# RWKV recurrence with two head pairs in step, mLSTM output projection in two rounds, and more row buffers, in a two-layer hybrid decoder step on one Trainium2 core

## The chip, the core and the metric

The kernel runs on one core of one Trainium2 chip. The engines that matter are TensorE (PE, with its weight loads shown as PEld), VectorE (DVE), ScalarE (ACT), GpSimd (POOL) and SyncE (SP), which here only issues DMAs. The metric is the device time of one execution in microseconds, the median of several runs.

## The reference

One inference step of a decoder trunk with two layers and D = 1024. A prompt of 512 tokens and 8 sample sequences of 4 tokens run through the same weights, so the kernel works on 544 columns. Each layer is a half SwiGLU (d_ff 2816), a mixer, and another half SwiGLU; mixer 0 is RWKV-7 time mixing (16 heads of 64), mixer 1 is mLSTM (8 heads, DV 128, DK 64). All is fp32.

```
def trunk(x, ...):
    for i in range(2):
        x = x + 0.5 * swiglu(rmsnorm(x), wg, wu, wd)       # "a"
        x = x + mixer_i(rmsnorm(x))
        x = x + 0.5 * swiglu(rmsnorm(x), wg, wu, wd)       # "b"
    return rmsnorm(x), states

def rwkv step(S, r_t, d_t, k_t, v_t, kk_t, b_t):           # per head, S is 64 x 64
    sa = S @ -kk_t
    S = S * d_t + outer(sa, b_t) + outer(v_t, k_t)
    return S, S @ r_t
# then group norm per head, + bonus, * gate, @ wo

def mlstm chunk(C, n, m):                                  # per head
    b = cumsum(logf); Dlog = b_t - b_s + logi_s, causal; m_t = max(b + m, max_s Dlog)
    S = (q k^T) * exp(Dlog - m_t)
    num = exp(b + m - m_t) * (C q) + S v; den likewise with n
    h = num / max(|den|, exp(-m_t))                        # then norm, * sigmoid(o), @ w_out
```

## The kernel before

Activations lie transposed, features on the 128 partitions and tokens along the row, in two parts of columns: PARTS[0] has 256 prompt tokens, PARTS[1] the other 256 and the 32 sample tokens. A dense product takes fp32 weights of 128 x 1024 from memory (`weight`, three raw buffers), splits them into a high and a low part (`split`: a copy on ScalarE, L341, and a subtraction on VectorE, L342) and multiplies in three matmuls (`mm3`, L345 to L347), 24 for one block of 128 output features and one part of columns. The instruction order on each engine comes from a planner that places ready work by priority in a simulated time line; work inside `high_priority` goes ahead of the dense work. PSUM has eight banks of 512 fp32 columns.

**The RWKV stage** runs beside dense work: SwiGLU "a" of part 1 and the projections of both parts, later the output projection and SwiGLU "b" of part 0 (`todo`, handed out by `step`; FILL and FILL2 say after which list entry how many units follow). Its recurrence works on head pairs (16 heads are 8 pairs of 128 partitions) and on 4 chunks of 64 tokens for each part, thus on 16 pairs in all, the second 8 starting from the state of the first. Pair n goes through:

- `rwkv_prep` (decays and scaled keys, bank `pq`),
- `rwkv_quad`: masked products of all four chunks (L907 on PE, mask L909 on DVE into `gm`), then the inverse of a unit triangular matrix by doubling in f16, with bursts of eight 64x64 matmuls (L928 to L960) that alternate with a copy (L938), an addition (L943) and a mask (L924); the result is `tf` (L962). Pairs alternate between two lanes, with one bank each (`b0`, `b1`); `gm`, `xt`, `tf`, `uv` have three buffers,
- `rwkv_tokens` (values transposed, bonus),
- `rwkv_chunk`, four times, each on the state of the one before: L1004/1007, copy L1009, L1012, copies L1013/1014, L1017, state L1022, output L1025/1028, copy L1029. Pair q and pair q - 1 run half a pair apart, each in a bank `pc` of its own,
- `rwkv_sample` in the second half: the 8 sample sequences of this pair, some 15 small products one after another (L1046 to L1100) that all go through the bank `ps`, of which there is one, and end in L1101 and the state's DMA,
- `rwkv_finish`: group norm and gate, three products (L1116, L1120, and the gate's up to L1133) in the bank of the other quad lane, up to L1134. In the second half it needs the sample's output (L1093).

The tiles of the sample recurrence lie in the scope `rw2`, whose memory comes free when the second half's projections (scope `rw1`) are done.

**The mLSTM stage** projects q and k for head pair j + 1 (`mlstm_qk`), while `mlstm_weights`, `mlstm_pair` and `mlstm_heads` work on pair j in banks of their own. `mlstm_weights` loads rows from memory broadcast to all partitions (`qi`, two buffers, L1345; `d`, four buffers, two per pair, L1353) and adds and masks them (L1356). Then come eight gates (`mlstm_gate`, dense, one `og` buffer each), eight products (`mlstm_out`) and the output projection (`project_out`), which for each of 8 output blocks and each part of columns sums over all eight heads and adds to x once (L501).

## Time and profile before

| what | us |
|---|---|
| median of 3 runs (2597.35 to 2598.86) | 2598.71 |
| profiled execution | 2593.75 |
| its span, first to last instruction | 2591.9 |

Durations are those of the profiled execution. L12 is line 12 of the kernel before. Stretches are given in us from the start of the span: dense SwiGLU "a" of part 0 to about 195, the RWKV stage to about 1238, dense work to 1862, the mLSTM stage to about 2176, dense work to the end. The granted clock is the mean share of full speed that PE was given; it has two levels, 1.2 and 2.4 GHz, so 0.75 means half of the time at the lower one. A matmul of fp32 shows as two records, of f16 or of the split parts as one. Matmuls overlap, so what one adds is the distance from its start to the next start, not its duration.

### The profile page before, as it was taken

The numbers are of one execution on the slowest core, as the hardware profiler recorded it, in microseconds if no ns is written. First come the engines' busy times: TensorE is split into PE (matmuls) and PEld (weight loads), VectorE is DVE, ScalarE is ACT, GpSimd is POOL, SyncE is SP. The second block draws the span as 40 slices with busy tenths as digits, with TensorE's granted clock in tenths as the row PEclk, the third lists the DMA queues.
The fourth block names the chain that finished last, engine by engine and source line by source line (L and its number), as shares of the span: only waits on it lengthen the run. The fifth ranks groups of instructions, "written<-read, shape, count | busy, mean of one in ns | idle before, by whom it ended". The sixth has DMA issues, their size and how long they took to land.

```text
span 2591.9 us, 54493 instructions
## 1 busy us (share of the span) xinstructions
PE 2512.9 (97%) x21731; PEld 2342.7 (90%) x21731; DVE 1583.3 (61%) x3266; ACT 1278.1 (49%) x2917; POOL 513.0 (20%) x578
## 2 busy tenths in 40 slices
PE   9998999999899999999999999999998999999997
PEld 8997998888788787889999999999977979999997
DVE  6667786778887687656766544443436645444433
ACT  6555665656666564545555533333335544333322
POOL 1204332332532243323121011110000000111100
PEclk9998999999899899999999999999998979999999
DMA  7564544233232232345555432322232312322232
GB/s 217 183 195 140 160 140 123 82 106 122 70 104 87 88 102 87 118 133 168 163 165 167 133 90 83 96 84 86 86 101 88 89 52 75 97 82 90 86 90 72
DMA packets 101070, 291.65 MB, mean 113 GB/s; under 512 B 12440, under 2 KB 28216, under 8 KB 100816
## 3 DMA queue, kind: packets, MB, share of 16 engines
q1 hardware_dynamic: 100816, 288.18, 36.5%
q8 instruction: 170, 2.79, 0.4%
q14 instruction: 84, 0.69, 0.1%
HBM read 278.76 MB, written 9.38 MB: 111 GB/s over the span
## 4 chain that ended last, share of the span: by engine, by line
PE 87%; DVE 8%; issue 1%; DMA 1%; ACT 1%; POOL 1%; SPq 0%; DVEq 0%; ACTq 0%; POOLq 0%
PE ps L345 17%; PE ps L347 17%; PE ps L346 17%; PE pd L345 7%; PE pd L346 7%; PE pd L347 7%; DVE wl L342 2%; DVE m L662 1%; PE ps L1209 1%; PE ps L1210 1%; PE pq L907 1%; PE ps L1211 1%; PE pc L1025 1%; PE b L907 1%; PE pc L1017 1%
## 5 line engine op out<-in xcount | busy, mean ns | idle before, releaser
L342 DVE TENSOR_TENSOR wl<-wr,wh 128x512 fp32r<-128x512 f32 (+2 forms) x1025 | 719.9, 704 | 482.2 <-ACT wh L341 458.6
L341 ACT CAST wh<-wr 128x512 fp32r<-128x512 f32 (+2 forms) x1025 | 622.6, 609 | 656.1 <-PE ps L346 419.4
L345 PE MATMUL ps<-a,wh 128*128 128x288 f32 (+1 forms) x2384 | 697.4, 293 | 11.0 <-ACT a L393 5.2
L347 PE MATMUL ps<-a,wl 128*128 128x288 f32 (+1 forms) x2384 | 694.0, 291 | 0.1
L346 PE MATMUL ps<-a,wh 128*128 128x288 f32 (+1 forms) x2384 | 687.3, 288 | 0.3
L345 PEld LDWEIGHTS ps<-a,wh 128*128 128x128 f32 x2384 | 452.3, 190 | 14.2 <-ACT a L393 5.7
L346 PEld LDWEIGHTS ps<-a,wh 128*128 128x128 f32 x2384 | 452.1, 190 | 2.3 <-DVE a L394 1.1
L347 PEld LDWEIGHTS ps<-a,wl 128*128 128x128 f32 x2384 | 449.9, 189 | 1.6 <-DVE wl L342 0.5
L417 POOL TENSOR_TENSOR t<-t,t 128x256 f32<-128x256 f32 (+1 forms) x132 | 141.6, 1073 | 862.4 <-ACT wh L341 404.9
L345 PE MATMUL ps<-h,wh 128*128 128x288 f32 (+1 forms) x1056 | 303.9, 288 | 0.0
L346 PE MATMUL ps<-h,wh 128*128 128x288 f32 (+1 forms) x1056 | 303.3, 287 | 0.0
L347 PE MATMUL ps<-h,wl 128*128 128x288 f32 (+1 forms) x1056 | 303.2, 287 | 0.0
L345 PE MATMUL pd<-rk,wh 128*128 128x288 f32 (+1 forms) x656 | 199.1, 304 | 5.8 <-DVE t L477 5.2
L346 PE MATMUL pd<-rk,wh 128*128 128x288 f32 (+1 forms) x656 | 198.7, 303 | 0.8 <-DVE rk L394 0.5
L347 PE MATMUL pd<-rk,wl 128*128 128x288 f32 (+1 forms) x656 | 199.0, 303 | 0.0
L347 PEld LDWEIGHTS ps<-h,wl 128*128 128x128 f32 x1056 | 198.9, 188 | 0.0
L346 PEld LDWEIGHTS ps<-h,wh 128*128 128x128 f32 x1056 | 198.9, 188 | 0.0
L345 PEld LDWEIGHTS ps<-h,wh 128*128 128x128 f32 x1056 | 198.6, 188 | 0.0
L341 ACT CAST h<-t 128x256 fp32r<-128x256 f32 (+1 forms) x132 | 55.3, 419 | 200.2 <-POOL t L417 200.2
L345 PEld LDWEIGHTS pd<-rk,wh 128*128 128x128 f32 x656 | 127.5, 195 | 9.6 <-ACT mx L663 2.9
L346 PE MATMUL pd<-mx,wh 128*128 128x256 f32 (+1 forms) x448 | 134.5, 301 | 1.4 <-DVE mx L664 1.3
L345 PE MATMUL pd<-mx,wh 128*128 128x256 f32 (+1 forms) x448 | 134.3, 301 | 0.7 <-ACT t L712 0.4
(406 smaller groups left out, 4731.2 us busy)
## 6 DMA issues: line engine op xcount, KB each, us to landing
wr<-in_f0a_u_dram SPq DMA_DIRECT2D x44, 512.0 KB, 3.5
wr<-in_f0b_g_dram SPq DMA_DIRECT2D x44, 512.0 KB, 3.5
wr<-in_f0b_u_dram SPq DMA_DIRECT2D x44, 512.0 KB, 3.5
wr<-in_f0a_g_dram SPq DMA_DIRECT2D x43, 512.0 KB, 3.5
wr<-in_f0b_d_dram SPq DMA_DIRECT2D x24, 512.0 KB, 3.6
wr<-in_f1a_g_dram SPq DMA_DIRECT2D x22, 512.0 KB, 3.4
wr<-in_f1a_u_dram SPq DMA_DIRECT2D x22, 512.0 KB, 3.5
wr<-in_f1b_g_dram SPq DMA_DIRECT2D x22, 512.0 KB, 3.5
```

The lines of the kernel that those rows point to most:

```text
L341: self.S.copy(dst_h, src)
L342: self.V.tensor_tensor(dst_l, src, dst_h, op=ALU.subtract)
L345: self.T.matmul(out, wh, xh, start=start, stop=False)
L346: self.T.matmul(out, wh, xl, start=False, stop=False)
L347: self.T.matmul(out, wl, xh, start=False, stop=stop)
L417: self.G.tensor_tensor(s, s, w, op=ALU.mult)
L662: V.scalar_tensor_tensor(m, d, self.vec("mu", c * 8 + k), xn, op0=ALU.mult, op1=ALU.add)
L907: T.matmul(pg[:, i * P:(i + 1) * P], xc[R[h], i].rearrange("p x t -> p (x t)"), arc[R[h], i].rearrange("p x t -> p (x t)"), start=True, st ...
L1017: T.matmul(pn[R[h], :64], xt[:, h * 64:(h + 1) * 64], uv[:, h, :], start=True, stop=True)
L1025: T.matmul(py[R[h], :64], uv[:, h, :], gm[:, 1 - h, 64:128], start=True, stop=st is None)
L1209: T.matmul(pss[q][:n, :], xs[k][0][:, ts], wt(cs)[0], start=k == 0, stop=False)
L1210: T.matmul(pss[q][:n, :], xs[k][0][:, ts], wt(cs)[1], start=False, stop=False)
```

## The change

Two head pairs go through the recurrence in step, as a double pair m (four for each half). `rwkv_quad` handles eight chunks at once: its bursts have 16 matmuls instead of 8, its ops twice the columns, and it writes one PSUM tile of two banks (`wide_bank`, one buffer) in place of the two lanes. The masked products of L907 alternate between the two heads, each with a bank. `rwkv_chunk` does one chunk of both pairs; its output gathers in a bank over the four chunks and is copied once. `rwkv_finish` takes the bank `ps`. Buffers change: `gm`, `xt`, `tf`, `uv` hold two double pairs; a2 tiles 10 instead of 8, mixing buffers 19 instead of 21; two more k projections come before the first quad, FILL and FILL2 stay. A double pair's quad is issued at the first chunk of the one before, its preparation two chunks later, the samples at the first two chunks, both finishes at the fourth.

In mLSTM the gates have six `og` buffers, heads 0 and 1 are multiplied before the last two gates, and the output projection runs in two rounds, over heads 0 to 3 and 4 to 7, each with half of the weights' columns and an addition to x of its own. `qi` has three buffers and `d` six.

```diff
@@ -26,10 +26,10 @@
 TT = TP + TS
 HA = TP // 2
-OFF=(20000,20000)
-SOFF = 20000
+OFF = 20000
+NMX = 19
 NT1 = 3
-NOG = 8
+NOG = 6
...
+ND = NPAIR // 2
+NA2 = 10
...
-            for k in range(KT):
+            for k in range(len(xs)):
                 c = slice(k * mw, (k + 1) * mw)
-                self.mm3(ps, *wt(c), xs[k][0][:, hs], xs[k][1][:, hs], k == 0, k == KT - 1)
+                self.mm3(ps, *wt(c), xs[k][0][:, hs], xs[k][1][:, hs], k == 0, k == len(xs) - 1)
...
-    def project_out(self, name, xs):
-        for m in range(KT):
-            def evac(i, hs, ps, m=m):
-                self.V.tensor_tensor(self.x[m][:, hs], ps, self.x[m][:, hs], op=ALU.add)
-            self.dense(self.a[name][m], xs, evac)
+    def project_out(self, name, xs, halves=1):
+
+        n = KT // halves
+        for ks in (range(h * n, (h + 1) * n) for h in range(halves)):
+            xk = [xs(k) for k in ks]
+            for m in range(KT):
+                def evac(i, hs, ps, m=m):
+                    self.V.tensor_tensor(self.x[m][:, hs], ps, self.x[m][:, hs], op=ALU.add)
+                self.dense(self.a[name][m][:, ks.start * P:ks.stop * P], xk, evac)
...
-                self.d, self.quad = {}, {}
-                self.chain = [self.bank("pc", 2) for _ in range(2)]
-                self.nhm = {"mx": 21, "hm": 8}
+                self.d, self.quad, self.st = {}, {}, {}
+                self.chain, self.chain_y = [self.bank("pc", 2) for _ in range(2)]
+                self.nhm = {"mx": NMX, "hm": 8}
...
-                    with self.tc.high_priority(OFF[0]):
-                        for n in (0, 1):
-                            self.rwkv_ahead(n)
-                            self.rwkv_square(n)
+                    with self.tc.high_priority(OFF):
+                        self.rwkv_ahead(0)
+                        self.rwkv_square(0)
                     for q, f in enumerate(second):
                         f()
                         self.step(FILL2.get(q, 0))
-                    with self.tc.high_priority(OFF[0]):
-                        for n in (0, 1):
-                            self.rwkv_value(n)
+                    with self.tc.high_priority(OFF):
+                        self.rwkv_value(0)
+                        self.rwkv_ahead(1)
                     first, second = self.rwkv_first(1)
                     self.todo += first
-                    self.rwkv_slots(0, 2 * NPAIR - 4)
+                    self.rwkv_slots(0, 10)
                     self.todo += second
-                    self.rwkv_slots(2 * NPAIR - 4, 2 * NPAIR)
+                    self.rwkv_slots(10, 16)
                 self.nhm = {"hm": 16}
                 with self.scope("rw2", nps=0):
-                    self.rwkv_slots(2 * NPAIR, 2 * NPAIR + 2)
+                    with self.tc.high_priority(OFF):
+                        self.rwkv_value(ND)
+                    self.rwkv_slots(16, 17)
                     self.todo += self.rwkv_out(0) + self.ffn_units(*after, 0)
-                    self.rwkv_slots(2 * NPAIR + 2, 4 * NPAIR + 2)
+                    self.rwkv_slots(17, 32)
...
-        return ([lambda: self.rwkv_norm(i)] + low[:4] + self.rwkv_project("r", 0, i) + k[:3],
-                k[3:] + low[4:] + self.rwkv_project("v", 3, i))
+        return ([lambda: self.rwkv_norm(i)] + low[:4] + self.rwkv_project("r", 0, i) + k[:5],
+                k[5:] + low[4:] + self.rwkv_project("v", 3, i))
...
+    def rwkv_value(self, m):
+        if m < 2 * ND:
+            uv = self.rp("uv", 2, [P, 1024]).rearrange("p (a c h v) -> p a c h v", a=2, c=4, h=2)
+            for a in range(2):
+                self.rwkv_tokens(2 * (m % ND) + a, m // ND, self.d[m][a]["v"], uv[:, a])
+            self.quad[m] += (uv,)
 
     def rwkv_slots(self, t0, t1):
 
+        for t in range(t0, t1):
+            m, c = divmod(t, 4)
+            i, j = divmod(m, ND)
+            with self.tc.high_priority(OFF):
+                if c == 0:
                     self.rwkv_square(m + 1)
+
+                    if m + 1 != ND:
+                        self.rwkv_value(m + 1)
+                if c == 2:
                     self.rwkv_ahead(m + 2)
+                if i and c in (0, 1):
+                    self.rwkv_sample(2 * j + c, self.d[m][c])
+                self.rwkv_chunk(m, c)
+                if c == 3:
+                    for a in range(2):
+                        self.rwkv_finish(2 * j + a, i, m)
+            self.step(-(-len(self.todo) // (t1 - t)))
...
+        return {"xc": xc, "xs": xs, "arc": arc, "ars": ars, "pc": pc, "y": k, "v": v}
+
+    def rwkv_quad(self, ds):
         V, S, G, T = self.V, self.S, self.G, self.T
         R = (slice(0, 64), slice(64, 128))
+        W = 8 * CH
+        pb = lambda: self.wide_bank()
+        h16 = lambda tag, w=W: self.rp(tag, 1, [P, w], F16)
+        q8 = lambda t: t[:, :W].rearrange("p (q t) -> p q t", q=8)
+        q4 = lambda t: t[:, :W].rearrange("p (a c t) -> p a c t", a=2, c=4)
+        wide = lambda m: m.unsqueeze(1).to_broadcast([P, 8, m.shape[-1]])
         em = lambda l: self.em16[:, l * CH:(l + 1) * CH]
         id16 = em(6)
         def each(f):
+            for q in range(8):
+                for g in range(2):
+                    f(R[g], slice(q * CH, (q + 1) * CH), slice(W + q * CH, W + (q + 1) * CH))
+        flat = lambda t: t.rearrange("p x t -> p (x t)")
+        gm = self.rp("gm", 2, [P, 2048]).rearrange("p (a c h t) -> p a c h t", a=2, c=4, h=2)
+        xt = self.rp("xt", 2, [P, 1024])
+        mask = self.maskg.unsqueeze(1).to_broadcast([P, 4, P])
+        for a, d in enumerate(ds):
+            xc, arc = d["xc"], d["arc"]
+            pg = pb()
             for i in range(4):
+                for h in range(2):
+                    T.matmul(pg[:, (1 - h) * 512 + i * P:(1 - h) * 512 + (i + 1) * P], flat(xc[R[h], i]), flat(arc[R[h], i]),
+                             start=True, stop=True)
+            for h in range(2):
+                V.tensor_tensor(gm[:, a, :, h, :], pg[:, h * 512:(h + 1) * 512].rearrange("p (c t) -> p c t", c=4), mask, op=ALU.mult)
+
+        for a, d in enumerate(ds):
+            px = self.bank("pq", 1)
             for i in range(4):
+                T.transpose(px[:, i * P:(i + 1) * P], flat(d["xc"][:, i]), self.ident)
+            S.copy(xt[:, a * 512:(a + 1) * 512], px)
...
-                V.tensor_tensor(both, both, pd, op=ALU.add)
-            else:
-                V.tensor_tensor(ti, ti, pd[:, :W], op=ALU.add)
+            for x in range(2 if l < 5 else 1):
+                z = slice(x * W, (x + 1) * W)
+                V.tensor_tensor(both[:, z], both[:, z], pd[:, z], op=ALU.add)
...
+    def wide_bank(self):
+        self.n += 1
+        return self.psum.tile([P, 1024], F32, tag="b", name=f"b_{self.n}", bufs=1)
...
+    def rwkv_chunk(self, m, c):
+        V, S, T = self.V, self.S, self.T
         R = (slice(0, 64), slice(64, 128))
+        gm, tf, xt, uv = self.quad[m]
+        ds = self.d[m]
+        st = self.st.get((m - ND) if c == 0 else m)
+        arc, pc = [d["arc"] for d in ds], [d["pc"][:, c:c + 1] for d in ds]
+        col = lambda a: slice(a * 64, (a + 1) * 64)
+        reg = lambda z: self.chain[:, z * P:(z + 1) * P]
+        pairs = [(a, h) for a in range(2) for h in range(2)]
         if st is not None:
+            sp = self.rp("sp", 1, [P, P])
+            for a in range(2):
+                S.activation(sp[:, col(a)], st[:, col(a)], AF.Copy, scale=pc[a])
+        pr, pu, pn = reg(c % 2), reg(2), reg(3)
+        for a in range(2):
             for h in range(2):
+                T.matmul(pr[R[1 - h], col(a)], gm[R[h], a, c, 1 - h, 0:64], uv[R[h], a, c, h, :], start=True, stop=st is None)
+            for h in range(2 if st is not None else 0):
+                T.matmul(pr[R[1 - h], col(a)], arc[a][R[h], c, 0, :], st[R[h], col(a)], start=False, stop=True)
+        rhs = self.rp("sm", 3, [P, P])
+        V.tensor_copy(rhs, pr)
+        for a in range(2):
+            for g in (1, 0):
+                T.matmul(pu[R[g], col(a)], tf[R[g], (a * 4 + c) * CH:(a * 4 + c + 1) * CH], rhs[R[g], col(a)], start=True, stop=True)
+        two = lambda t: t.rearrange("p (a v) -> p a v", a=2)
+        V.tensor_copy(uv[R[1], :, c, 0, :], two(pu[R[1]]))
+        S.copy(uv[R[0], :, c, 1, :], two(pu[R[0]]))
+        for a, h in pairs:
+            z = (a * 4 + c) * P + h * 64
+            T.matmul(pn[R[h], col(a)], xt[:, z:z + 64], uv[:, a, c, h, :], start=True, stop=True)
+        sn = self.rp("stp", ND, [P, P]) if m < ND and c == 3 else self.rp("sm", 3, [P, P])
+        for a in range(2):
+            if st is None:
+                V.tensor_scalar(sn[:, col(a)], pn[:, col(a)], pc[a], None, op0=ALU.mult)
+            else:
+                V.scalar_tensor_tensor(sn[:, col(a)], pn[:, col(a)], pc[a], sp[:, col(a)], op0=ALU.mult, op1=ALU.add)
+        out = lambda a: slice(a * 4 * CH + c * CH, a * 4 * CH + (c + 1) * CH)
+        py = self.chain_y
+        for a in range(2):
             for h in range(2):
+                T.matmul(py[R[h], out(a)], uv[:, a, c, h, :], gm[:, a, c, 1 - h, 64:128], start=True, stop=st is None)
+            for h in range(2 if st is not None else 0):
+                T.matmul(py[R[h], out(a)], st[R[h], col(a)], arc[a][R[h], c, 1, :], start=False, stop=True)
+        if c == 3:
+            for a in range(2):
+                S.copy(ds[a]["y"][:, :HA], py[:, a * HA:(a + 1) * HA])
+        self.st[m] = sn
...
-        pb = lambda: self.bank(f"b{(j + 1) % NSTREAM}", 1)
+        pb = self.ps
...
-                ogs = [self.mlstm_gate(h, xs, rs) for h in range(8)]
-                ys = [self.mlstm_out(h, og) for h, og in enumerate(ogs)]
-                self.project_out("m_out", ys)
+                ogs = [self.mlstm_gate(h, xs, rs) for h in range(NOG)]
+                ys = [self.mlstm_out(h, ogs[h]) for h in range(8 - NOG)]
+                ogs += [self.mlstm_gate(h, xs, rs) for h in range(NOG, 8)]
+                self.project_out("m_out", lambda h: ys[h] if h < len(ys) else self.mlstm_out(h, ogs[h]), 2)
...
-        qi = self.unit("qi", 2)
+        qi = self.unit("qi", 3)
...
-        wS = [self.unit("d", 4) for _ in range(2)]
+        wS = [self.unit("d", 6) for _ in range(2)]
```

## Rows read from the trace of the kernel before

**Rows 1.** The page: busy microseconds by engine, and TensorE's granted clock in 40 slices.

```profile
PE 2512.9 (97%) x21731; PEld 2342.7 (90%) x21731; DVE 1583.3 (61%) x3266; ACT 1278.1 (49%) x2917; POOL 513.0 (20%) x578
...
PEclk9998999999899899999999999999998979999999
```

**Rows 2.** Table by stretches: PE, PEld, DVE, ACT, POOL busy; clock, DMA, GB/s.

```profile
398.00:640.00 242.00, 237.62 (x2694) 206.17 (x2688) 182.89 (x392) 145.99 (x372) 75.49 (x90) 0.99 0.35 106
640.00:824.00 184.00, 169.88 (x1731) 147.86 (x1731) 151.00 (x318) 116.66 (x312) 68.50 (x94) 0.91 0.30 92
824.00:1184.00 360.00, 353.27 (x3882) 293.60 (x3881) 250.80 (x593) 198.84 (x515) 119.74 (x137) 0.96 0.35 106
...
1238.00:1862.00 624.00, 623.13 (x4863) 622.43 (x4861) 317.10 (x575) 258.44 (x492) 71.52 (x72) 1.00 0.38 116
...
1982.00:2007.00 25.00, 15.86 (x87) 11.25 (x83) 14.86 (x58) 15.01 (x53) 2.04 (x2) 0.71 0.31 100
...
2097.00:2126.00 29.00, 26.75 (x106) 17.64 (x106) 12.67 (x48) 11.09 (x50) 2.52 (x2) 0.58 0.17 51
2126.00:2176.00 50.00, 49.42 (x381) 48.95 (x380) 31.39 (x62) 22.12 (x46) 0.00 (x0) 0.97 0.24 75
```

**Rows 3.** Timeline of PE, 912 to 916 us: start, duration, instruction.

```profile
912.10 0.28 PE L347 MATMUL pd<-xs,wl 128*128 128x256 f32 x1
912.31 0.31 PE L936 MATMUL b<-ti,e 64*64 64x64 f16 x8
912.55 0.75 PE L1120 MATMUL b<-a,c_c_rw 128*128 128x288 f32 x2
...
915.35 0.31 PE L940 MATMUL b<-p1s,ti 64*64 64x64 f16 x8
915.49 0.29 PE L942 MATMUL b<-ti,p1s 64*64 64x64 f16 x8
915.71 0.41 PE L345 MATMUL b<-a,a 128*128 128x288 f32 x1
```

**Rows 4.** Timeline of PE, the same product in two orders.

```profile
569.09 1.16 PE L907 MATMUL b<-a 64*128 64x128 f32 x8
570.17 0.33 PE L1012 MATMUL pc<-sm,tf 64*64 64x64 f32 x4
...
1958.41 1.16 PE L1365 MATMUL pS<-q,k 64*128 64x128 f32 x16
1959.50 0.44 PE L1393 MATMUL px<-c_c_all,k 128*128 128x128 f32 x2
```

**Rows 5.** Two lines of the sample recurrence: ns min/median/max, first and last start.

```profile
L1101 DVE TENSOR_TENSOR s<-s,ps x8: 686/688/689, 866.2 to 1180.4; 128x512 f32<-128x512 f32 x8
...
L1048 DVE TENSOR_TENSOR sa<-ps,c_c_rw x16: 205/216/217, 824.0 to 1142.5; 64x64 f32<-64x64 f32 x16
```

**Rows 6.** First mask and last op of the quads, same columns.

```profile
L909 DVE TENSOR_TENSOR gm<-b,c_c_rw x16: 660/691/692, 338.2 to 1063.3; 128x512 f32<-128x512 f32 x16
...
L962 DVE TENSOR_TENSOR tf<-ti,b x16: 402/419/422, 398.4 to 1117.9; 128x256 f32<-128x256 f16 x16
```

**Rows 7.** Timelines of PE, ACT and DVE: one rwkv_finish; then its last line.

```profile
908.98 0.75 PE L1116 MATMUL b<-rk,c_c_rw 128*128 128x288 f32 x2
...
910.07 0.42 ACT L1118 ACTIVATE a<-b 128x288 f32<-128x288 f32 x1
...
913.34 0.50 ACT L756 ACTIVATE a<-b,epsc 128x288 f32<-128x288 f32 x1 [0.31 <-PE b L1120]
...
918.24 0.45 DVE L1134 TENSOR_TENSOR rk<-rk,b 128x288 f32<-128x288 f32 x1
...
L1134 DVE TENSOR_TENSOR rk<-rk,b x16: 410/430/455, 479.2 to 1185.0; 128x256 f32<-128x256 f32 x8, 128x288 f32<-128x288 f32 x8
```

**Rows 8.** DVE in mLSTM: a wait for rows; the projection's evacuations.

```profile
1992.81 0.62 DVE L1356 SCALAR_TENSOR_TENSOR d<-d,cols,c_c_ml 128x128 f32<-128x128 f32 x2 [1.58 <-DMA d<-dc]
...
L501 DVE TENSOR_TENSOR x<-ps,x x16: 424/437/458, 2132.7 to 2176.1; 128x256 f32<-128x256 f32 x8, 128x288 f32<-128x288 f32 x8
```

More of the change, by code (lines that the diff above doesn't have):

```diff
@@ L640, in rwkv_norm @@
         else:
-            t = [self.rp("gm", 3, [P, 1024]) for _ in range(2)]
-            self.dx = [t[k // 4][:, k % 4 * HA:(k % 4 + 1) * HA] for k in range(KT)]
+            t = self.rp("gm", 2, [P, 2048])
+            self.dx = [t[:, k * HA:(k + 1) * HA] for k in range(KT)]
         sub = lambda *t: self.G.tensor_tensor(*t, op=ALU.subtract)
@@ L759, in act, with rwkv_ahead @@
         return r
-    def rwkv_ahead(self, n):
-        if n < 2 * NPAIR:
-            self.d[n] = self.rwkv_prep(n % NPAIR, n // NPAIR)
-    def rwkv_square(self, n):
-        if n < 2 * NPAIR:
-            self.quad[n] = self.rwkv_quad(n, self.d[n])
-    def rwkv_value(self, n):
-        if n < 2 * NPAIR:
-            self.quad[n] += (self.rwkv_tokens(n, self.d[n]),)
-    def rwkv_slots(self, t0, t1):
-        jobs = [(t, q) for t in range(t0, t1) for q in (t // 2 - 1, t // 2) if 0 <= q < 2 * NPAIR]
-        ahead = lambda q: self.tc.high_priority(OFF[q // NPAIR] if q < 2 * NPAIR else SOFF)
-        for z, (t, q) in enumerate(jobs):
-            m = t // 2
-            if t % 2 == 0 and t and (q == m - 1 or m == 0):
-                with ahead(min(m + 1, 2 * NPAIR - 1)):
+    def rwkv_ahead(self, m):
+        if m < 2 * ND:
+            self.d[m] = [self.rwkv_prep(2 * (m % ND) + a, m // ND) for a in range(2)]
@@ L795, in rwkv_slots @@
-            with ahead(q):
-                self.rwkv_chunk(t - 2 * q, self.quad[q], self.d[q], q % 2)
-                if t - 2 * q == 3:
-                    self.rwkv_finish(q % NPAIR, q // NPAIR)
-            self.step(-(-len(self.todo) // (len(jobs) - z)))
+                if i and c in (0, 1):
[4 more added lines that the diff above has]
+                        self.rwkv_finish(2 * j + a, i, m)
@@ L911, in rwkv_quad @@
-        px = self.bank("pq", 1)
-        for i in range(4):
-            T.transpose(px[:, i * P:(i + 1) * P], xc[:, i].rearrange("p x t -> p (x t)"), self.ident)
-        xt = self.rp("xt", 3, [P, 4 * P])
-        S.copy(xt, px)
+            for q in range(8):
[3 more added lines that the diff above has]
+        gm = self.rp("gm", 2, [P, 2048]).rearrange("p (a c h t) -> p a c h t", a=2, c=4, h=2)
```

107 lines of the change are left out of this document (18 added, 89 removed).

## Prediction, made before the changed kernel ran

> **What bounds the kernel now.** I read the page first: busy shares and the clock [rows 1]. TensorE (PE) is busy 97% of a 2591.9 us span and the chain that ends last is mostly PE, so only three things can move the time: PE work that is dearer than it need be, PE idle time, and time at the lower of its two clock levels (1.2 instead of 2.4 GHz). The table by stretches shows where each lies [rows 2]. The pure dense stage, 1238 to 1862 us, runs 4863 matmuls in 624 us at granted clock 1.00: 0.128 us each and nothing to gain. The RWKV stage, up to 1238, and the mLSTM stage behind 1862 differ: matmuls come faster than the dense rate but small ones are mixed in, PE idles 14 us in 640 to 824 with the clock at 0.91, and in 2097 to 2126 the clock is 0.58. So the change is costed in those two stages, against the profiled execution (2593.75 us, of which the span is all but 1.85). The median of the runs shown is 4.96 us above that; I add this at the end.
>
> **RWKV: fewer, longer bursts on PE.** The timeline of PE shows what a small burst costs between dense matmuls [rows 3]. Dense instructions follow each other at 0.12 to 0.13 us. The 8 f16 matmuls of L936 start 0.21 us after the last dense one and the next group starts 0.24 us later; 16 in a row (L940 with L942) take 0.36 us to the next start. So 8 more in the same burst cost 0.12 us, while a burst of its own costs 0.24 plus the 0.09 lost ahead of it. Two pairs in one step put two bursts together wherever the code issued one for each pair: 14 per pair in the quad (L928 to L960) and 4 per chunk step (L1004/1007, L1012, L1017, L1025/1028), thus (16 x 14 + 64 x 4) / 2 = 240 bursts fewer. Each saves 0.21 us if it stood alone among dense work and next to nothing if it stood in a row of small bursts; bounds 0 and 50 us. I take 0.1 us, since most of these bursts have another small one beside them: 24 us.
>
> **RWKV: the mask products.** L907 is re-ordered: the head h now alternates inside the loop over chunks, with the two heads in two banks. The trace has both orders in the same form, 64x128 on 64 rows [rows 4]: L907 with one head in a row takes 1.08 us to the next start for 8 records (4 matmuls), L1365 with heads alternating takes 1.09 us for 16 records (8 matmuls). So a pair's 8 matmuls cost 1.09 instead of 2.17 us: 16 x 1.08 = 17 us of PE.
>
> Together 41 us of PE work, about half of it on either side of 824 us. Against it in the first half: the fill table FILL2 keeps its positions although the list it indexes lost two entries, and the mixing has 19 buffers instead of 21, so one product instead of two can be prepared ahead at each of twelve hand-overs. Nothing shows these; nearest is the idle time of the mixing stretch 640 to 824, 14 us, so 0 to 14 us, and I take 3 (recurrence work covers most of it). The first half gains 20.5 - 3 = 17.5 us, and the point where samples may start (the first L1048 ran at 824.0 [rows 5], when the second half's projections had freed their tiles) moves to 807.
>
> **RWKV: is the single quad lane too slow?** One lane takes the place of two. The first quad took from the first mask at 338.2 to its L962 at 398.8, 61 us [rows 6]; the 16 quads, two in flight, ended from 398.8 to 1118.3, which is 48.0 us each or 96 for two pairs. In step, the ops double: a 128x512 op takes 0.69 us and a 128x256 one 0.42. Ten ops of the chain get some 0.27 us longer and six get a second instruction of 0.69: 7 us. 68 us is under 96, so this lane doesn't set the pace.
>
> **RWKV: what is late next.** The sample recurrences do. The first runs from 824.0 (its L1048) to 866.9 (its L1101), and the eight L1101 go on to 1180.4 [rows 5], 44.9 us apart: a sample takes 43 us and its successor starts at once, so they stand in a chain, through the one bank `ps`. Until now rwkv_finish used the quad's banks; the change puts its three products into `ps` too. A finish holds its bank for 908.98 to 910.49, 912.55 to 913.84 and 915.71 to 918.69: 5.8 of its 9.7 us [rows 3, 7]. Each second of `ps` that a finish holds, a sample waits, unless it falls into one of the sample's stretches without a bank (between its ops on SBUF, on GpSimd, and its load). Bounds: nothing, and the full 9.7 us for each of eight. I take half of the hold, 3 us, because the list of ready work lets a finish slip between two products of a sample. The stage then ends at 807 + 8 x 44.9 + 8 x 3 + 10 (two finishes at the end, in series; the last one's rest ran from 1180.4 to 1185.4 [rows 5, 7]) + 25 (the output projection that needs them, 192 matmuls of 0.128) = 1225 instead of 1238. The other 28 us of dense work that stood behind 1185 move into the chain's gaps. RWKV: **-13 us**. PE's work alone would have ended at 1238 - 17.5 - 20.5 = 1200, so some 25 us of the gain are lost to this chain.
>
> **mLSTM: the projection in two rounds.** In 2097 to 2126 PE has only small matmuls: 26.75 of 29 us busy at clock 0.58, and then the output projection's 384 matmuls come alone [rows 2]. At full clock the 29 us would hold 29 x 0.58 = 16.8, and less the idle 2.25 it is 14.5 us of work. The first round needs heads 0 to 3 alone, 192 matmuls, 24.6 us, and fits beside them. What is saved is 29 - 14.5 = 14.5 us; below nothing only if the gates, now with six buffers, wait for the first two products, which depend on the first pair of heads alone. The 16 more evacuations cost 16 x 0.437 = 7 us on VectorE [rows 8], hidden in 2126 to 2176, where it is busy 31 of 50 us. Weight transfers become twice as many of half the size; three buffers ahead of PE cover them, and if that cover went, ScalarE would show waits on them.
>
> **mLSTM: buffers for the rows.** For 1.58 us ahead of 1992.81 VectorE waits for rows of the third pair's weights [rows 8], which could not be loaded until the first pair released a buffer; behind it on the same engine stand the state updates, for which PE waits: 1982 to 2007 has 9 us idle and clock 0.71. With a third set the load comes early. Worth 0 to 13 us; I take 3, since VectorE's and ScalarE's own work fills most of that stretch. mLSTM: **-17.5 us**.
>
> **Rivals.**
> (a) *The chain of samples hides less than I think, and PE's gain shows whole.* If finishes cost the samples nothing and samples get shorter as PE gets emptier, RWKV ends at 1200: -38 - 17.5 = -55.5, 2543 us. For it: a finish only holds a bank for parts of its time. Against: samples run back to back now.
> (b) *Slower: the bank `ps` becomes the stage's bound.* With x us lost for each of eight finishes the stage ends at 1201 + 8x. RWKV's gain is gone at x = 4.6, the whole gain at x = 6.8; at the full 9.7 us it ends at 1279, +23 us in all. With x = 8.2, 2610 us (2599 to 2622). For it: one buffer, and ops in order. Against: the hold of 5.8 us is under 6.8.
> (c) *Slower by the clock.* Where PE waits on evictions between small bursts its clock falls: 0.58 in 2097 to 2126, 0.71 in 1982 to 2007, 0.91 in 640 to 824 [rows 2]. With one quad lane there is no second lane to fill PE. If all of 398 to 1184 (0.957 on the mean of its three rows) ran at 0.91, its 752 us of full-clock work would need 827 us, +41, and 2609 us in all. The Trainium skill has such a rule: "TensorE: Matmul & The Clock Gate", section "A second HAM failure mode: psum-queue depth-cycling", says that a kernel which cycles PSUM banks each iteration lets PE idle briefly so often that the clock swings between its levels. By that rule the single bank pair would cost; the trace agrees so far as the clock is below 1.00 in every stretch with such bursts, but it stays at 0.96 to 0.99 where dense work stands between them, and that work remains.
> (d) *It doesn't matter.* Bursts already hidden, the projection's gates not ready in time: 2594 to 2604.
>
> **How the numbers follow.** Span 2591.9 - 13 - 17.5 = 2561.4; with 1.85 around it and 4.96 to the median, **2568 us**. Chances: forecast 0.50 (its own range 2555 to 2590), (a) 0.22, (b) 0.13, (c) 0.05, (d) 0.10. Measurement tells some 0.2% apart, 5 us: faster 0.73 (forecast, (a) and a little of (d)), same 0.09, slower 0.18. The range takes in (a) with the bound of the row buffers and half of (b): 2530 to 2615.
>
> **What would show it.** Right: L907 takes about 1.1 us for 16 records; bursts of 16 f16 matmuls; L1101 48 us apart or less, the last at about 1190; the clock near 1.00 where the last mLSTM pair runs, with matmuls of the projection among its small ones; no VectorE wait on the rows. Wrong: L1101 more than 51 us apart (rival b), clock under 0.95 in 398 to 1184 (c), or a dry PE ahead of 807 because of the mixing.

## The result and the profile after

The changed kernel took 2578.23 us (median; 2575.27 to 2581.44) against 2598.03 for the kernel before on the same chip: ratio 0.9924, 95% interval 0.9907 to 0.9941, so 19.8 us or 0.76% faster. The forecast was 2568 us, in a range of 2530 to 2615. The direction came, but 10 us of the gain did not, and the traces show that one of the two stages gave all of it.

The profiled execution after took 2580.45 us (before: 2593.75). Executions of one kernel differ by 6 us and more here, so the 13.3 us between the two traces and the 19.8 between the medians are the same result, and shifts of a stretch below are good to a few microseconds.

The page after, busy time by engine and the granted clock of TensorE (PE) in 40 slices:

```profile
PE 2476.4 (96%) x21731; PEld 2323.5 (90%) x21731; DVE 1583.1 (61%) x3178; ACT 1258.1 (49%) x2772; POOL 497.6 (19%) x514
...
PEclk9999999999789899998999999999998979999999
```

PE does the same 21731 matmuls in 36.5 us less than in [rows 1]. The table by stretches says where that went (columns as in [rows 2]: PE, PEld, DVE, ACT, POOL busy; clock, DMA, GB/s):

```profile
640.00:808.00 168.00, 145.55 (x1239) 130.21 (x1240) 140.14 (x278) 107.67 (x267) 57.52 (x76) 0.87 0.31 94
808.00:1180.00 372.00, 361.96 (x4286) 312.94 (x4285) 267.38 (x570) 204.77 (x480) 125.64 (x127) 0.98 0.40 119
1180.00:1222.00 42.00, 34.05 (x182) 27.44 (x182) 19.42 (x40) 16.29 (x33) 2.07 (x2) 0.76 0.28 84
1222.00:1846.00 624.00, 622.50 (x4859) 621.83 (x4858) 317.14 (x577) 259.10 (x492) 71.50 (x76) 1.00 0.38 116
...
2083.00:2116.00 33.00, 31.01 (x120) 21.97 (x121) 15.83 (x53) 12.06 (x50) 2.49 (x2) 0.53 0.16 50
2116.00:2163.00 47.00, 46.30 (x367) 45.83 (x365) 33.20 (x71) 19.95 (x41) 0.00 (x0) 1.00 0.30 96
2163.00:2579.00 416.00, 400.15 (x3176) 399.10 (x3176) 176.87 (x319) 134.75 (x259) 49.00 (x50) 0.98 0.28 85
```

The pure dense stage is the yardstick: 4859 matmuls in 622.5 us at clock 1.00, as in 1238 to 1862 before [rows 2], now from 1222. So **RWKV ends 16 us earlier**. The closing stretch of 3176 matmuls starts at 2163; before it started at 2176:

```profile
2176.00:2592.00 416.00, 400.09 (x3176) 399.10 (x3176) 175.60 (x316) 133.10 (x255) 48.94 (x50) 0.98 0.28 85
```

That is 13 us earlier, so **mLSTM gained nothing** (the 3 us that it lost are within what such shifts can tell): the last pair runs at clock 0.53 (2083 to 2116) as it ran at 0.58 before. Two places in RWKV stand out, too: 640 to 808 has 22 us without PE work at clock 0.87 (14 us at 0.91 in [rows 2]), and 1180 to 1222, which was solid dense work before, is at clock 0.76 with 8 us idle.

**Why that end is so thin.** VectorE's timeline after, three lines of the sample and the finish (L1111 ends a sample, as L1101 before; L1144 ends a finish, as L1134; L1058 starts a sample, as L1048):

```profile
893.44 0.69 DVE L1111 TENSOR_TENSOR s<-s,ps 128x512 f32<-128x512 f32 x1 [0.58 <-PE ps L1110]
903.51 0.45 DVE L1144 TENSOR_TENSOR rk<-rk,ps 128x288 f32<-128x288 f32 x1
915.01 0.45 DVE L1144 TENSOR_TENSOR rk<-rk,ps 128x288 f32<-128x288 f32 x1
919.74 0.21 DVE L1058 TENSOR_TENSOR sa<-ps,c_c_rw 64x64 f32<-64x64 f32 x1
...
1196.97 0.69 DVE L1111 TENSOR_TENSOR s<-s,ps 128x512 f32<-128x512 f32 x1 [3.53 <-PE ps L1110]
1204.37 0.46 DVE L1144 TENSOR_TENSOR rk<-rk,ps 128x288 f32<-128x288 f32 x1
1211.36 0.46 DVE L1144 TENSOR_TENSOR rk<-rk,ps 128x288 f32<-128x288 f32 x1
```

Sample, finish, finish, and only then the next sample: 26 us pass between the end of one pair of samples and the start of the next, against 3 to 4 us between the two samples of a pair. The same holds at 1002.0 and 1100.8. At the end both finishes stand behind the last sample, and the last output projection behind them.

### The profile page after: what moved, and what is told of

It is laid out like the page before. It is cut to its first block, busy times and chain, and to the rows that moved or that the text cites. A ratio compares the mean times of both kernels' runs of the same rounds, so it can differ in the third digit from the quotient of the medians.

```text
span 2578.7 us, 54194 instructions
## 1 busy us (share of the span) xinstructions
PE 2476.4 (96%) x21731; PEld 2323.5 (90%) x21731; DVE 1583.1 (61%) x3178; ACT 1258.1 (49%) x2772; POOL 497.6 (19%) x514
## 4 chain that ended last, share of the span: by engine, by line
PE 85%; DVE 9%; issue 2%; ACT 2%; DMA 1%; POOL 1%; SPq 0%; DVEq 0%; ACTq 0%; POOLq 0%
PE ps L346 17%; PE ps L348 17%; PE ps L347 17%; PE pd L346 7%; PE pd L347 7%; PE pd L348 7%; DVE wl L343 2%; DVE m L668 1%; PE ps L1220 1%; PE ps L1221 1%; PE ps L1222 1%; PE b L912 1%; PE ps L1110 1%; PE pc L1034 1%; DVE mx L670 1%
```

## The experiments

Ratios are to the kernel before on the same chip; the changed kernel's own is 0.9924.

**1. Another bank for the finishes.**

```diff
 def rwkv_finish(self, j, i, m):
-        pb = self.ps
+        pb = lambda: self.bank("pq", 1)
```

> The changed kernel, with one edit: the three products of rwkv_finish take the bank pq instead of ps. Theory A: a bank is handed out in program order, so the first product of the next pair's sample waits until both finishes of the step before have had ps; that is the 26 us between L1111 at 893.4, 1002.0, 1100.8 and the next L1058 at 919.7, 1026.8, 1127.1, and the finishes of the last step wait in the same way for the last sample (its L1111 at 1197.0). With another bank the samples stand at most 5 us apart, the last L1111 comes before 1165, PE becomes the bound again and the stage ends 13 to 20 us earlier: 2558 to 2566 us. Theory B, PE work and the chunk steps set the end and the gap between samples costs nothing: 2573 to 2583. Theory C, finishes in pq hold back quads and preparation, which use it: above 2583.

Measured: 2563.78 us (2558.20 to 2569.62), ratio 0.9872 (0.9854 to 0.9890), 13.5 us less than the changed kernel by the ratios and 20.9 by the profiled executions. VectorE's timeline at the same place, then two stretches:

```profile
874.46 0.69 DVE L1111 TENSOR_TENSOR s<-s,ps 128x512 f32<-128x512 f32 x1 [1.17 <-PE ps L1110]
877.86 0.21 DVE L1058 TENSOR_TENSOR sa<-ps,c_c_rw 64x64 f32<-64x64 f32 x1
...
799.00:1150.00 351.00, 341.14 (x4098) 287.08 (x4096) 250.83 (x556) 195.77 (x466) 113.76 (x118) 0.98 0.36 111
1150.00:1201.00 51.00, 50.51 (x409) 49.85 (x409) 35.68 (x67) 30.68 (x61) 10.74 (x12) 1.00 0.56 172
```

The hole between samples is 3.4 us instead of 26, the last L1111 runs at 1149.6 instead of 1197.0, the end of the stage is solid dense work at full clock again, and the dense stage starts at 1201. That is the 1200 that the prediction had named as PE's own limit. Theory A holds. Not all of the 21 us are the holes, though: the first sample, too, started earlier, at 798.4 instead of 806.9 (at 798.4 to 801.8 in the traces of experiments 1, 6, 7 and 9, which all have this edit, 804.7 with 21 mixing buffers; the cause is not shown). And the samples, with finishes beside them again, took 40.8 us each (first L1058 to L1111, mean of eight) instead of 37.5.

**2. The same bank, finishes issued later.** In the second half:

```diff
+                if i and j and c == 1:
+                    for a in range(2):
+                        self.rwkv_finish(2 * j - 2 + a, i, m - 1)
                 self.rwkv_chunk(m, c)
-                if c == 3:
+                if c == 3 and not (i and j < ND - 1):
```

> The changed kernel, with the bank ps kept, but in the second half the two finishes of a step are issued after the second sample of the following step instead of before the first. Theory A (order of the bank): the same 26 us gaps between pairs of samples go, three of them, while the finishes of the last step still wait for the last sample; the last L1111 comes 30 to 60 us earlier, the time is 2560 to 2568. Theory B (PE work and chunk steps set the end): 2573 to 2583.

Measured: 2586.18 us, ratio 0.9957 (0.9945 to 0.9970), some 8 us *slower* than the changed kernel. Theory A in this form failed. A move in the program order only moves the place in the line: at the end four finishes stand in it instead of two, as VectorE's timeline of this kernel shows (L1114 ends a sample, L1147 a finish):

```profile
1192.23 0.69 DVE L1114 TENSOR_TENSOR s<-s,ps 128x512 f32<-128x512 f32 x1 [2.09 <-PE ps L1113]
1199.06 0.45 DVE L1147 TENSOR_TENSOR rk<-rk,ps 128x288 f32<-128x288 f32 x1
...
1219.90 0.46 DVE L1147 TENSOR_TENSOR rk<-rk,ps 128x288 f32<-128x288 f32 x1
```

The last L1147 comes 8.5 us later than the last L1144 at 1211.4. Two holes of 29 and 25 us are left between the samples, and the last sample came only 4.7 us earlier instead of 30 to 60. The new order moved the charge; it didn't remove it.

**3. The finishes put into ps in the kernel before, alone.**

```diff
 def rwkv_finish(self, j, i):
-        pb = lambda: self.bank(f"b{(j + 1) % NSTREAM}", 1)
+        pb = self.ps
```

> The kernel before, with one part of the change alone: rwkv_finish takes its three products from the bank ps instead of the quad's banks. Theory A (samples and finishes wait for each other in the order in which ps is handed out): the eight samples can't follow each other in 44.9 us any more; with 10 to 13 us for each finish, less what a sample gets shorter, the last L1101 comes 15 to 60 us later and the time is 2610 to 2650 us. Theory B (a finish slips into the pauses of a sample, 3 us each or less, and the dense work behind hides it): 2595 to 2608.

Measured: 2606.85 us, ratio 1.0043 (1.0031 to 1.0055): 11 us slower. That is inside theory B's span, at its upper end, but the samples show theory A's mechanism. Their last line, ns min/median/max, first and last start:

```profile
L1101 DVE TENSOR_TENSOR s<-s,ps x8: 669/687/690, 871.8 to 1228.0; 128x512 f32<-128x512 f32 x8
```

They end (1228.0 - 871.8) / 7 = 50.9 us apart instead of 44.9 [rows 5]: **6.0 us for each finish, net**. That this is near the 5.8 us for which a finish holds its bank is chance, as VectorE's timeline shows, before and then with this edit:

```profile
909.09 0.69 DVE L1101 TENSOR_TENSOR s<-s,ps 128x512 f32<-128x512 f32 x1
913.59 0.22 DVE L1048 TENSOR_TENSOR sa<-ps,c_c_rw 64x64 f32<-64x64 f32 x1 [2.09 <-PE ps L1046]
```

```profile
1135.34 0.69 DVE L1101 TENSOR_TENSOR s<-s,ps 128x512 f32<-128x512 f32 x1 [1.02 <-PE ps L1100]
1146.49 0.46 DVE L1134 TENSOR_TENSOR rk<-rk,ps 128x288 f32<-128x288 f32 x1
1149.96 0.22 DVE L1048 TENSOR_TENSOR sa<-ps,c_c_rw 64x64 f32<-64x64 f32 x1
```

From one L1101 to the next L1048 it took 4.2 us before and takes 15.5 now (means of seven): the hole grows by **11.3 us for each finish**, more than the 9.7 that a finish takes from its first product to its last line [rows 7]. Against that the samples, with no finish beside them, got shorter: 36.1 us from the first L1048 to L1101 instead of 40.9 (means of eight). In PE's timeline of this stretch no product of a sample stands between the three of a finish (1138.58 to 1146.15). The last sample comes 48 us later, but the time grew by only 11, since dense work had stood behind the chain.

**4. The mLSTM part undone.** In the changed kernel:

```diff
-NOG = 6
+NOG = 8
-        qi = self.unit("qi", 3)
+        qi = self.unit("qi", 2)
-        wS = [self.unit("d", 6) for _ in range(2)]
+        wS = [self.unit("d", 4) for _ in range(2)]
...
-                self.project_out("m_out", lambda h: ys[h] if h < len(ys) else self.mlstm_out(h, ogs[h]), 2)
+                self.project_out("m_out", lambda h: ys[h])
```

> The changed kernel, with the mLSTM part undone: projection in one round, eight gate buffers, two sets of row buffers. Theory A: the two rounds and the third set gave nothing, since the first round began only behind the last pair and the wait for rows went over to the fourth pair's rows: 2574 to 2580 us. Rival, the step as predicted (14.5 + 3 us gained, and lost elsewhere): 2590 to 2598.

Measured: 2579.86 us, ratio 0.9936 (0.9923 to 0.9948), the same as with it within the noise. Two rounds and a third set of rows together are worth nothing that shows, as they stand.

**5. Buffers of their own for the first round.** Where the first round waited, timelines of ScalarE and VectorE in the changed kernel say: the high part of head 0 is there at 2086.84, its low part not before 2110.97.

```profile
2086.84 0.64 ACT L342 CAST hi<-q 128x544 fp32r<-128x544 f32 x1 [0.39 <-DVE q L1341]
2110.56 0.58 ACT L1477 COPY q<-po 128x512 f32<-128x512 f32 x1 [2.50 <-PE po L1479]
2110.97 0.71 DVE L343 TENSOR_TENSOR q<-q,hi 128x544 fp32r<-128x544 f32 x1
```

The low part takes a buffer named q, and so does the last pair's output (L1477), which stands ahead of it in the program. So:

```diff
 def mlstm_out(self, h, og):
-        hi, lo = self.rp("hi", 8, [P, TT], F32R), self.rp("qk"[h % 2], 5, [P, TT], F32R)
+        lo = self.rp("lo", 4, [P, TT], F32R) if h < 4 else self.rp("qk"[h % 2], 5, [P, TT], F32R)
+        hi = self.rp("hi", 8, [P, TT], F32R)
-NOG = 6
+NOG = 4
```

and two sets of rows again, as in experiment 4, to make room.

> The changed kernel, with buffers of their own (four) for the low parts of the first four heads' outputs, which took theirs from the q and k buffers; to make room, four gate buffers instead of six, and two sets of row buffers again instead of three. Theory A: the low part of head 0 (L343 at 2110.97) waited because a buffer of that name is handed out in program order and the last pair's own output (L1477 at 2110.56) stood ahead of it; with its own buffer the first round of the projection runs beside the last pair: clock near 1.00 there instead of 0.53, the stretch from the end of RWKV to the next dense stage 12 to 18 us shorter, 2560 to 2567 us. Theory B: VectorE and ScalarE set the pace of the last pair, the projection's work only moves: 2573 to 2583.

Measured: 2569.33 us, ratio 0.9890 (0.9875 to 0.9905), 8.9 us less than the changed kernel. Its VectorE line and two stretches:

```profile
2043.74 0.66 DVE L343 TENSOR_TENSOR lo<-q,hi 128x544 fp32r<-128x544 f32 x1
...
2083.00:2125.00 42.00, 40.10 (x271) 33.73 (x270) 24.45 (x75) 17.10 (x58) 2.49 (x2) 0.95 0.26 84
2125.00:2150.00 25.00, 24.75 (x187) 24.51 (x186) 20.90 (x46) 15.42 (x33) 0.00 (x0) 0.94 0.33 96
```

The low part is written 67 us earlier, the last pair runs at clock 0.95 among 271 matmuls, and only the second round (187) is left behind it. Theory A holds in mechanism; the gain is 9 instead of 12 to 18 us. The edits that make room (gates, rows) were not run by themselves.

**6. The rows of the next pair.** In the changed kernel the third pair's rows are loaded early, yet VectorE waits at the same place, now for the fourth pair's:

```profile
1979.25 0.61 DVE L1367 SCALAR_TENSOR_TENSOR d<-d,cols,c_c_ml 128x128 f32<-128x128 f32 x2 [1.40 <-DMA d<-dc]
```

That was 1.58 us at this point in [rows 8]. To take it out of the way of the state updates, the weights were issued behind the pair, in the kernel with both repairs (experiment 7; it has two sets of rows again, so that the wait there is the third pair's, 1.36 us ahead of 1963.97):

```diff
-                        if j < 3:
-                            self.mlstm_weights(j + 1)
                         self.mlstm_pair(j)
                         self.mlstm_heads(j)
+                        if j < 3:
+                            self.mlstm_weights(j + 1)
```

> The kernel with both repairs, and the weights of the next mLSTM pair issued behind the pair and its heads instead of ahead of them, so that the wait of VectorE for rows (1.40 us ahead of 1979.25 in the changed kernel) and the masks behind it do not stand ahead of the state updates and the heads' chain for which PE waits. Theory A (that wait and what is behind it cause the stall with half clock at 1978 to 1999): 4 to 12 us less than the kernel with both repairs, 2540 to 2548. Theory B (the chain of the pair itself causes it): within 3 us of it. Theory C (the next pair then starts later): above 2556.

Measured: 2550.05 us, ratio 0.9828 (0.9815 to 0.9840), against 0.9826: no difference. The stretch of the stall, first with both repairs, then with this edit on top:

```profile
1937.00:1995.00 58.00, 48.51 (x346) 41.62 (x344) 29.48 (x90) 25.33 (x83) 2.03 (x2) 0.85 0.23 73
```

```profile
1937.00:1995.00 58.00, 56.88 (x343) 45.63 (x342) 31.35 (x101) 30.85 (x115) 4.60 (x4) 0.82 0.26 82
```

The idle time went from 9.5 to 1.1 us, but the clock stayed low and as many matmuls ran in the 58 us: PE was spread out, not faster. The wait itself didn't go, it moved (1.03 us ahead of 1958.92); what is shown is that the idle time behind it was worth nothing measurable. The rows as a cause are not tested further.

**7. Both repairs together** (experiments 1 and 5).

> The changed kernel with both repairs: finishes in the bank pq, and buffers of their own for the low parts of the first four heads (four gate buffers, two sets of rows). The two lie in stages that follow each other, so theory A (independent) gives the sum of both, 13 to 14 us and 9: 2553 to 2559 us. Theory B (one of them had gained by a run-to-run shift): above 2562.

Measured: 2552.23 us (2550.22 to 2553.89), ratio 0.9826 (0.9813 to 0.9839). The ratios of the two repairs would add to 0.9838, so they are independent within the noise. It is the fastest of the versions, along with experiment 6 and the second of experiment 10, which are equal to it: 1.7% below the kernel before and 1% below the changed one.

**8. The order of the heads.** Groups of the mask products by line (busy us, mean ns | idle ahead), first before, then after:

```profile
L907 PE MATMUL pq<-a 64*128 64x128 f32 x128 | 21.8, 315 | 4.5 <-DVE a L877 2.4 <-DVE rk L982 2.1
L907 PE MATMUL b<-a 64*128 64x128 f32 x128 | 21.4, 307 | 0.4 <-DVE a L877 0.4
```

```profile
L912 PE MATMUL b<-a 64*128 64x128 f32 x256 | 23.7, 290 | 0.5 <-DVE a L879 0.2
```

Two kernels were to say how much of this is the order. In the kernel before, the order alone:

```diff
-        for h in range(2):
-            pg = self.bank("pq", 1) if h else pb()
-            for i in range(4):
+        pgs = [self.bank("pq", 1) if h else pb() for h in range(2)]
+        for i in range(4):
+            for h, pg in enumerate(pgs):
```

> The kernel before, with one part of the change alone: in the mask products the head alternates inside the loop over chunks, its two heads in their two banks (b and pq). Theory A (PE work sets the pace there, as the step on the mask products has it): a pair's eight matmuls take 1.1 us instead of 2.17, 17 us of PE work over sixteen pairs; the half ahead of the first sample shows whole (8.5), the half behind it at most in part, since the samples of before follow each other in 44.9 us anyway: 2580 to 2590 us. Theory B, the two products run into other waits (both banks must be free at once): no change, 2594 to 2600.

Measured: 2603.48 us, ratio 1.0027 (1.0017 to 1.0038), slightly slower. PE's timeline shows that it did not test the order:

```profile
882.08 2.05 PE L907 MATMUL pq<-a 64*128 64x128 f32 x8 [2.01 <-DVE rk L983]
911.24 1.16 PE L907 MATMUL b<-a 64*128 64x128 f32 x8
```

The heads' two banks come free at different times, so each head still ran in a row, eight records by themselves, and PE waited more for pq (4.8 us in 824 to 1190 instead of 2.1). In the changed kernel, the old order:

```diff
-            for i in range(4):
-                for h in range(2):
+            for h in range(2):
+                for i in range(4):
```

> The changed kernel, with the old order of the mask products: one head in a row, then the other. PE work grows by 17 us. Theory A (the second half of the stage is bound by the order of samples and finishes through ps, not by PE): only the 8.5 us ahead of the first sample show, 2583 to 2591 us. Theory B (PE sets the pace of both halves): 2592 to 2598. Theory C (the order of the heads is worth nothing in time): 2574 to 2582.

Measured: 2587.59 us (2581.57 to 2589.63), ratio 0.9959 (0.9946 to 0.9971), 9 us slower. Its group, and one burst in PE's timeline with the start behind it:

```profile
L912 PE MATMUL b<-a 64*128 64x128 f32 x256 | 29.4, 286 | 0.1
...
511.21 1.71 PE L912 MATMUL b<-a 64*128 64x128 f32 x16
512.85 0.70 PE L989 MATMUL pq<-rk,c_c_rw 128*128 128x256 f32 x2
```

By busy time the order is worth 29.4 - 23.7 = 5.7 us of PE; by the distance to the next start, which is what a burst adds, 1.64 - 1.09 = 0.55 us for each of 16 pairs, 8.8 us. The time that it moved, 9 us, is near the second figure and inside the span of theory A; with so much less than 17 us of work, the split into halves that the theory speaks of can't be read from it.

**9. The fill table.** On top of both repairs:

```diff
-FILL2 = {5: 3, 6: 3, 9: 4}
+FILL2 = {3: 3, 4: 3, 7: 4}
```

> As the kernel with both repairs, and the positions of the table FILL2 moved down by the two entries that its list lost (5, 6, 9 become 3, 4, 7). Theory A (the misplaced fill leaves PE waiting for mixed inputs in 640 to 800, where it idles 18 us and the clock is 0.87): 2 to 8 us less than the kernel with both repairs alone. Theory B (the waits there come from the mixing itself, with 19 buffers, and from the last chunks of the first half): within 2 us of it.

Measured: 2555.38 us, ratio 0.9838 (0.9825 to 0.9852), no gain over 0.9826 (3 us slower, within the spread of its runs). The table's positions cost nothing.

**10. Buffers of the mixing.** Fewer, in the changed kernel:

```diff
-NMX = 19
+NMX = 17
```

> The changed kernel with 17 buffers for mixed inputs instead of 19 (before had 21). Theory A (the two buffers that the change took cost the 6 us by which waits for mx in 640 to 808 grew): two more cost the like again, 2582 to 2592 us. Theory B (the waits for mx come from other things, the order in which the mixing is issued): 2575 to 2582.

Measured: 2589.16 us, ratio 0.9979 (0.9970 to 0.9988), 11 us slower by the medians and 14 by the ratios. Its first sample, ns min/median/max, first and last start:

```profile
L1058 DVE TENSOR_TENSOR sa<-ps,c_c_rw x16: 204/210/218, 815.4 to 1183.7; 64x64 f32<-64x64 f32 x16
```

It starts 8.5 us after the changed kernel's 806.9. More buffers, with both repairs, paid for with a tile of the quads' preparation:

```diff
-NMX = 19
+NMX = 21
-NA2 = 10
+NA2 = 9
```

> The kernel with both repairs, with 21 buffers for mixed inputs instead of 19 as before the change; the room comes from the tiles of the quads' preparation, nine instead of ten. Theory A (the buffers that the change gave up cost what 17 instead of 19 cost, 8 us ahead of the first sample, or some of it): 3 to 8 us less than the kernel with both repairs, 2544 to 2549 us. Theory B (19 were enough once finishes no longer take ps, and the tenth preparation tile is worth as much): within 3 us of it or above.

Measured: 2552.71 us, ratio 0.9831 (0.9818 to 0.9845): no difference. Two fewer cost; whether 21 alone would gain is open, since the tile given up for them may take back what the buffers give.

## Why the prediction was right and wrong, step by step

**Fewer bursts and the mask products (24 + 17 = 41 us of PE): right in sum.** PE is busy 36.5 us less than before. The groups of the quads' f16 bursts, before and then after:

```profile
L936 PE MATMUL b<-ti,e 64*64 64x64 f16 x640 | 27.1, 199 | 2.7 <-DVE ti L943 2.2 <-DVE ti L931 0.4
L940 PE MATMUL b<-p1s,ti 64*64 64x64 f16 x640 | 27.6, 199 | 1.9 <-ACT p1s L938 1.9
L942 PE MATMUL b<-ti,p1s 64*64 64x64 f16 x512 | 20.9, 197 | 0.0
```

```profile
L942 PE MATMUL b<-ti,e 64*64 64x64 f16 x640 | 18.8, 196 | 1.5 <-DVE ti L951 1.4
L946 PE MATMUL b<-p1s,ti 64*64 64x64 f16 x640 | 18.0, 197 | 0.4 <-ACT p1s L944 0.4
L948 PE MATMUL b<-ti,p1s 64*64 64x64 f16 x512 | 13.8, 195 | 0.0
```

75.6 us became 50.6 for the same matmuls. (Such groups overlap their neighbours, so the sum of all of them is more than the 36.5.) The mask products lost 43.2 - 23.7 = 19.5 us in their rows, near the 17. But the reason was only partly the order: by busy time experiment 8 leaves 5.7 us to it and 13.8 to the longer run. PE's timeline gives both prices by starts:

```profile
587.70 1.16 PE L912 MATMUL b<-a 64*128 64x128 f32 x16
588.79 0.27 PE L1034 MATMUL pc<-gm,uv 128*64 128x64 f32 x1
```

Sixteen records take 1.09 us to the next start, as forecast. In a row, one head and then the other, they take 1.64 (experiment 8), and eight of one head alone 1.08 [rows 4]; so 2 x 1.08 - 1.64 = 0.52 us are saved by running the two heads' bursts one behind the other, and 0.55 by alternating: by this measure the two halves are about equal, 8.3 and 8.8 us for 16 pairs. The prediction put all of the difference down to the order. The Trainium skill, "TensorE: Matmul & The Clock Gate", section "The mechanism", says that weight loads overlap running matmuls only when the row group differs; the trace agrees here, 1.09 us with alternating halves of the rows against 1.64 in a row. As a rule for all loads the trace does not bear it out: in the pure dense stage, where every load takes all 128 rows, PEld is busy for 621.83 us beside PE's 622.50.

**The first half (-17.5, first sample at 807): right in the number, by two errors that cancel, which is luck.** The first L1058 ran at 806.9. But up to there PE was busy 27.7 us less (the table's stretches from the start to 824 and to 808, summed), not 20.5 (a part of that is work left for later: 7309 matmuls instead of 7462 lie ahead of this point), and idle 11.7 us more, not 3. So the sign "a dry PE ahead of 807" came. Most of the idle time stands ahead of products that take mixed inputs, as the costliest group of them shows, before and then after:

```profile
L346 PE MATMUL pd<-mx,wh 128*128 128x256 f32 (+1 forms) x448 | 134.5, 301 | 1.4 <-DVE mx L664 1.3
```

```profile
L347 PE MATMUL pd<-mx,wh 128*128 128x256 f32 (+1 forms) x448 | 135.5, 304 | 9.5 <-DVE mx L670 6.6 <-POOL mx L670 2.8
```

The term of 3 us for this idle time was mis-sized, within its bounds of 0 to 14. Not all of the 11.7 us is the mixing's: with finishes in another bank (experiment 1) PE was idle only 7.6 us more than before, up to 799. Of the two causes named, the fill table is out (experiment 9), and 19 buffers are on a slope on which two fewer cost 8.5 us at this point (experiment 10); that 21 instead of 19 would give as much was not shown, and the one run with 21 gained nothing.

**The single quad lane sets no pace: right.** The last quad ended at 1060.0 instead of 1117.9 [rows 6].

**The chain through ps becomes the bound: right, and its end nearly so (1222 against 1225), but with wrong parts.** L1111 are (1197.0 - 857.7) / 7 = 48.5 us apart, where 47.9 was forecast and 51 was to count as wrong. The step that failed is "the list of ready work lets a finish slip between two products of a sample": finishes stand in the line whole. In the changed kernel, too, the two of a step open a hole of 25.8 us (mean of three) where 3.3 us lie between two samples of a pair, 11.3 us for each finish as in experiment 3, instead of 3, and above the bound of 9.7. It did not show in the spacing because the samples themselves got shorter: 37.5 us from the first L1058 to L1111 (mean of eight) instead of 40.9. The prediction held them at 44.9 with their hand-over. PE's lighter load is not the reason that the traces suggest: with finishes in another bank they take 40.8 us beside the same PE work (experiment 1), and 36.1 in the old kernel with finishes in `ps` (experiment 3). They are short where no finish runs beside them; this fits all four traces, but no run tests it alone. The sum has a slip, too: it charges eight finishes to the samples and the last two once more as 10 us, though only six stand between samples. The last L1111 came at 1197, 7 us behind the forecast's 1190, and what stands behind it took 25 us instead of 35: the end time is right by luck.

Rival (a) is what happens to RWKV without the line: experiment 1 ends the stage at 1201, the 1200 of that rival. Rival (b), that the chain eats the whole gain, needed 6.8 us a finish at an unchanged sample; the hole was larger than that, but the sample did not stay as it was: against experiment 1 the time from the first L1058 to the last L1111 is 390.1 instead of 351.2 us, net 6.5 for each of six finishes.

**The projection in two rounds (-14.5): wrong, nothing came.** The sentence that failed is that the first round "needs heads 0 to 3 alone". It also needs four buffers, and those were named like the last pair's outputs, which come first in the program. I had looked at the gates as the only bound. Experiment 5 shows the mechanism with that removed, and its size: 9 us rather than 14.5. The clock reached 0.95 and 0.94 instead of 1.00, and VectorE is busy 20.9 of the 25 us behind the pair; which of them keeps the rest was not tested.

**The third set of rows (-3): wrong, nothing that shows.** The third pair's load came early as forecast, but the fourth pair's masks moved up into its place on VectorE and waited 1.40 us. Even with the idle time behind such a wait gone (experiment 6, with two sets) the time did not move. A gain of 3 us by itself would be hard to tell from the noise.

**The clock (rival (c)): did not come.** 808 to 1180 ran at 0.98, against 0.96 before in 824 to 1184. The rule of the Trainium skill that the prediction weighed there ("TensorE: Matmul & The Clock Gate", section "A second HAM failure mode: psum-queue depth-cycling") does not show in this stretch. The clock is low where PE idles or has little dense work: 0.87 in 640 to 808, with 22 us idle, 0.76 in 1180 to 1222 and 0.53 in 2083 to 2116. The mean of the three stretches from 398 to 1180 is 0.96, as in the prediction's 0.957 before.

**Sum.** Forecast -13 in RWKV and -17.5 in mLSTM; the traces show -16 and +3. The range, which reached to the rivals on both sides, held it. So the forecast was right in its direction and its range, and half right in its reasons: the RWKV stage gave what was forecast by parts that cancel, and the mLSTM stage gave none of its 17.5.

## What to carry to other kernels

A buffer or bank with one name is a queue in program order: before work is counted as "can run beside", list every buffer that it takes and who stands ahead of it under that name, results included. When a user is added to a bank, charge its whole run, from its first take of the bank to its last release, to everybody behind it (11 us here, not the 5.8 of its holds); what others gain by running without it beside them has to be measured. Moving it in the order only moved the charge here, another bank removed it. When a wait is taken away by one more buffer, look which instruction of the same kind moves up into the place.

## What was not expected

Eight mask records of one head take 1.08 us alone, sixteen of two heads 1.64 in a row and 1.09 alternating. Idle time of PE was no measure of loss in a stretch at low clock: in experiment 6, 8.4 us less idle in 58 us moved no time. And a version with both repairs is at 2552.23 us, ratio 0.9826, by small edits of names and buffer counts: the change's own bank and buffer names had kept a part of its gain from showing.
